# Gate projections as narrow fp32 strips, and the context stream moved behind the latent stream in the opening of a hybrid layer

## The chip, the cores and the metric

The kernel runs on one core of one Trainium2 chip. The metric is the device time of one execution, in microseconds. Three runs of the kernel before took 936.86, 937.15 and 937.77 us, so the median is 937.15 us.

## The reference, cut to what matters

One layer of a diffusion backbone works on 512 latent tokens (`x`, 512 by 1024) and 256 context tokens (`ctx`, 256 by 1024). Everything is float32. What the change touches is the opening of the layer:

```python
mod   = silu(c)     @ w_ada + b_ada            # shift, scale, gate vectors of the latents
mod_c = silu(c_ctx) @ w_ada + b_ada            # the same for the context
h  = rms_norm(x,   g_norm1) * (1 + sc1)  + sh1
hc = rms_norm(ctx, g_norm1) * (1 + csc1) + csh1
aq, ak, av, dq, dk, dv, dz, da, db, ga, gd = split_cols(h @ w_in)      # and the same of hc
beta = sigmoid(db)                             # 16 columns: 2 directions x 8 heads
g    = -exp(a_log) * softplus(da + dt_bias)    # 16 columns
q, k, v = silu(conv3(dq, dk, dv)); k = l2_normalize(k) ...
# gated delta rule in chunks of 64 tokens, forward and backward, the context's final state into the latents;
# windowed attention beside it; both gated, projected, then an MLP of width 4096
```

`da` and `db` are the gate projections: 16 columns each of a combined projection of 4896 columns. `dk` has 512 columns, four tiles of 128, and its latents and context tokens both go through a short convolution, a SiLU and a normalization before the triangular matrices of the delta rule can be built.

## The kernel before, in words

Activations lie transposed: 128 channels on the partitions, tokens along the free axis, eight channel groups (`KT = 8`). A projection to 128 output columns is a tile. Each weight tile (512 KB) is loaded raw, then split into a rounded part (`hi`, line 240, ScalarE) and the rest (`lo`, line 241, VectorE); activations are split the same way (lines 295 and 296). `mm3` (lines 289 to 291) adds three fp32r products per channel group: hi by hi, hi by lo, lo by hi. So a tile of the latents is 24 products of 512 columns, and its context part 24 products of 256 columns. They accumulate in PSUM, which has eight banks of 512 columns, handed out in a ring; `bank(2)` takes two neighbours.

The opening. `NONES` products of a matrix of ones (line 188) come first. The latents (`xT`, four loads of 512 KB) and context (`ctxT`, two) are squared (line 265, ScalarE), added up on VectorE (lines 269 and 273) and summed over the partitions by a product with ones (line 276); a Ln and an Exp give the reciprocal root. `ada(kt)` computes shift and scale of channel group `kt` as a row: two loads of 512 KB of `w_ada`, and for each four products of 32 output rows by 256 columns (line 207) that lie side by side in the array's four column groups; in plain fp32 each product shows as two records. `columns(kt)` copies the row out (line 221), turns it into columns with two small products (line 226) and forms `modA` and `modS` (lines 229 and 230). `modulate` then does, for latents and for context, a product with the reciprocal root and the scale on VectorE (line 294), the rounded part with the shift added on ScalarE (line 295) and the rest on VectorE (line 296).

Three tiles are early: the gate tile (`T_AB`, where 32 of 128 columns are in use) and the first two tiles of `dk`. Their products run inside the loop over channel groups, for latents and context, as each group is modulated:

```python
early, EARLY = [], {T_AB: 0, T_DK: 0, T_DK + 1: 0}
        if kt + AHEAD < KT:
            columns(kt + AHEAD, ada(kt + AHEAD))
        for (w, acc), k0 in zip(early, EARLY.values()):
            for k in range(kt + 1) if kt == k0 else (kt,):
                mm3(acc[:, :512], w, [hx[k]], ...)
                mm3(acc[:, 512:768], w, [hc[k]], ...)
```

After the loop come constants, then the gates (lines 601 to 624: a chain of small operations on ScalarE and VectorE over 768 tokens on 16 partitions that ends in `gb` at line 622), the other two tiles of `dk`, the convolutions (lines 573 to 575), the SiLU of all four, and the products that bring `gb` into token order (line 649). From there `mats` (normalization, line 591, then the chunk matrices, lines 699 to 731) runs woven with the projections for attention, and the triangular matrices are inverted row by row on VectorE.

The order of each engine's instructions is fixed when the kernel is built: the framework's planner takes, for every engine, the ready instruction that stands earliest in the program, by its own estimate of durations, and puts in the waits. A NoSync dependency (`tc.add_manual_dep`) adds an order without a semaphore. `act` keeps activations that share a function table together: a group with another table starts after all of the group before. All loads are issued by SyncE in one queue. SBUF outside the pools is a ring of 167 units of 256 columns (`alloc`); a reused unit makes the next writer wait for its last reader. Raw weight tiles have four buffers, split ones two.

## Time and profile before

| | |
|---|---|
| median of three runs | 937.15 us (936.86 to 937.77) |
| the profiled execution's own time | 938.35 us |
| its span, first to last instruction | 936.5 us |
| TensorE (PE) busy | 901.0 us, 96% |
| VectorE (DVE) busy | 596.2 us, 64% |
| ScalarE (ACT) busy | 443.0 us, 47% |
| mean granted clock of TensorE | 0.991 |

Busy time of PE is not PE at its peak, since products overlap and their ends are modelled: how long a product costs is read from the distance between the starts of neighbours. PEld are the weight loads that run beside. DMA share 1.0 means that all 16 DMA engines had work all the time. PEclk is the granted clock: 1.00 is 2.4 GHz and 0.50 is 1.2 GHz.

### The profile page before, as it was taken

What the parts mean: (1) busy time and instruction counts of PE and PEld (TensorE: products, weight loads), DVE (VectorE), ACT (ScalarE), POOL (GpSimd) and SP (SyncE); (2) the same over time, 40 slices, a digit from 0 to 9 for tenths busy, and PEclk for the clock granted to TensorE, in tenths of its full rate; (3) what the DMA queues carried; (4) which work ended last, traced back from release to release, by engine and by line L of the source; (5) the groups of instructions that cost most, each with busy time, mean ns of one, the idle gap of its engine ahead of it and who ended that gap; (6) DMA issues with size and microseconds to landing.
All of it is one profiled execution on the core that took longest, in us unless ns stands there. A gap on an engine that the chain in (4) does not pass through costs nothing.

```text
span 936.5 us, 18158 instructions
## 1 busy us (share of the span) xinstructions
PE 901.0 (96%) x7736; PEld 730.0 (78%) x7736; DVE 596.2 (64%) x1013; ACT 443.0 (47%) x815; POOL 12.1 (1%) x26
## 2 busy tenths in 40 slices
PE   7999889999999999989999998999999999999998
PEld 5688667877777677778888888988888888888886
DVE  4666779997877998358875977982454235434411
ACT  5467635338567887475555434660243125213400
POOL 0000000000000001000000000000000000000000
PEclk8999989999999999999999999999999999999999
DMA  9921111210000132225424474481344124222111
GB/s 350 347 69 46 47 47 46 68 46 24 23 11 24 34 114 92 93 92 162 157 86 136 157 273 137 143 291 39 115 152 138 45 68 156 92 67 91 45 43 47
DMA packets 29600, 98.72 MB, mean 105 GB/s; under 512 B 3664, under 2 KB 4176, under 8 KB 29520
## 3 DMA queue, kind: packets, MB, share of 16 engines
q1 hardware_dynamic: 29520, 97.57, 31.5%
q8 instruction: 60, 0.98, 0.4%
q14 instruction: 20, 0.16, 0.1%
HBM read 95.46 MB, written 2.10 MB: 104 GB/s over the span
## 4 chain that ended last, share of the span: by engine, by line
PE 72%; DVE 12%; ACT 8%; DMA 4%; issue 3%; SPq 0%; DVEq 0%; ACTq 0%
PE banks L289 16%; PE banks L290 15%; PE banks L291 15%; PE banks L943 9%; PE banks L988 2%; DMA wr<-in_wm 2%; PE banks L1055 2%; DMA wa<-in_wada 2%; DVE wl L241 1%; ACT m L146 1%; PE banks L1086 1%; PE banks L1067 1%; PE banks L526 1%; DVE m L183 1%; PE banks L207 1%
## 5 line engine op out<-in xcount | busy, mean ns | idle before, releaser
L289 PE MATMUL banks<-m,m 128*128 128x512 f32 (+1 forms) x584 | 219.4, 379 | 3.4 <-ACT m L240 3.0
L290 PE MATMUL banks<-m,m 128*128 128x512 f32 (+1 forms) x584 | 219.0, 377 | 0.1
L291 PE MATMUL banks<-m,m 128*128 128x512 f32 (+1 forms) x584 | 218.9, 377 | 0.0
L240 ACT ACTIVATE m<-wr 128x1024 fp32r<-128x1024 f32 x67 | 70.8, 1058 | 157.9 <-PE banks L290 78.9
L289 PEld LDWEIGHTS banks<-m,m 128*128 128x128 f32 x584 | 109.2, 188 | 26.4 <-ACT m L240 3.1
L241 DVE TENSOR_TENSOR m<-wr,m 128x1024 fp32r<-128x1024 f32 x67 | 81.9, 1224 | 70.3 <-PE banks L290 34.2
L290 PEld LDWEIGHTS banks<-m,m 128*128 128x128 f32 x584 | 109.5, 188 | 21.7 <-DVE m L241 0.8
L291 PEld LDWEIGHTS banks<-m,m 128*128 128x128 f32 x584 | 109.3, 188 | 21.2 <-issue 0.8
L289 PE MATMUL banks<-m,wh 128*128 128x512 f32 (+1 forms) x312 | 114.1, 366 | 0.9 <-DVE m L1270 0.6
L291 PE MATMUL banks<-m,wl 128*128 128x512 f32 (+1 forms) x312 | 111.5, 360 | 2.3 <-DVE wl L241 2.3
L290 PE MATMUL banks<-m,wh 128*128 128x512 f32 (+1 forms) x312 | 111.0, 356 | 0.0
L943 PE MATMUL banks<-m,wh 128*128 128x512 f32 x320 | 103.9, 399 | 0.0
L1371 DVE SCALAR_TENSOR_TENSOR m<-banks,modT,m 128x512 f32<-128x512 f32 x32 | 24.0, 750 | 101.0 <-PE banks L291 101.0
L241 DVE TENSOR_TENSOR wl<-wr,wh 128x1024 fp32r<-128x1024 f32 (+1 forms) x60 | 64.7, 1079 | 28.4 <-ACT wh L240 28.2
L240 ACT ACTIVATE wh<-wr 128x1024 fp32r<-128x1024 f32 (+1 forms) x60 | 56.6, 944 | 31.5 <-PE banks L290 15.0
L943 PEld LDWEIGHTS banks<-m,wh 128*128 128x128 f32 x320 | 59.1, 188 | 12.1
L291 PEld LDWEIGHTS banks<-m,wl 128*128 128x128 f32 x312 | 58.8, 189 | 11.3 <-DVE wl L241 3.0
L289 PEld LDWEIGHTS banks<-m,wh 128*128 128x128 f32 x312 | 59.3, 190 | 10.4 <-DVE m L1270 0.8
L290 PEld LDWEIGHTS banks<-m,wh 128*128 128x128 f32 x312 | 59.3, 190 | 7.5 <-issue 0.2
L943 PE MATMUL banks<-m,wl 128*128 128x512 f32 x160 | 65.0, 406 | 0.0
L182 ACT ACTIVATE m<-m 128x512 fp32r<-128x512 f32 (+1 forms) x56 | 35.2, 631 | 48.9 <-DVE m L1354 21.1
L183 DVE TENSOR_TENSOR m<-m,m 128x512 fp32r<-128x512 f32 (+1 forms) x56 | 38.3, 689 | 18.8 <-ACT m L182 18.3
(231 smaller groups left out, 1274.7 us busy)
## 6 DMA issues: line engine op xcount, KB each, us to landing
wr<-in_wm SPq DMA_DIRECT2D x64, 512.0 KB, 3.5
wr<-in_win SPq DMA_DIRECT2D x39, 512.0 KB, 3.5
wa<-in_wada SPq DMA_DIRECT2D x32, 512.0 KB, 4.0
m<-in_wada SPq DMA_DIRECT2D x16, 512.0 KB, 10.2
m<-in_xT SPq DMA_DIRECT2D x8, 512.0 KB, 6.1
wr<-in_wbr SPq DMA_DIRECT2D x16, 256.0 KB, 2.7
wr<-in_wout SPq DMA_DIRECT2D x8, 512.0 KB, 4.7
out<-m SPq DMA_DIRECT2D x8, 256.0 KB, 2.0
```

The lines of the kernel that those rows point to most:

```text
L146: r = A.activation(out_, in_, func, **kw)
L182: A.activation(r32(hi), src, AF.Copy)
L183: (eng or V).tensor_tensor(r32(lo), src, hi, op=ALU.subtract)
L240: A.activation(r32(hi), raw, AF.Copy)
L241: V.tensor_tensor(r32(lo), raw, hi, op=ALU.subtract)
L289: PE.matmul(acc, w[0][:, k, :], xhi, start=(start and i == 0), stop=False)
L290: PE.matmul(acc, w[0][:, k, :], xlo, start=False, stop=False)
L291: PE.matmul(acc, w[1][:, k, :], xhi, start=False, stop=(stop and i == n - 1))
L943: PE.matmul(acc.ap, w[x][:, k, :], hx[k][y], start=(k == p == 0), stop=(k == KT - 1 and p == 2))
L988: PE.matmul(pa.ap, w[x][:, j, :], r32(Q[y][:, :, j, :]), start=(j == p == 0), stop=(j == 3 and p == 2))
L1055: PE.matmul(z[r, x * 256 + q * HD:x * 256 + (q + 1) * HD], src[q][r, col(c):col(c) + CH], S[r, q * HD:(q + 1) * HD], start=True, stop=True)
L1371: V.scalar_tensor_tensor(xn_[ct], acc.ap, modT[:, 3, ct:ct + 1], xn_[ct], op0=ALU.mult, op1=ALU.add)
```

## The change

- The gate tile is gone from the list of tiles. Its 32 used columns become a weight `wab` of 128 KB. For each channel group one plain fp32 product of 32 output rows is formed; four groups lie side by side in the four column groups of the array and give four partial sums in one bank, which ScalarE and VectorE add up later, with `da` and `db` on 32 neighbouring partitions. ScalarE writes an fp32 copy of each modulated group for it.
- All four tiles of `dk` are early, one bank each, and only their latents are multiplied beside the modulation. The context's loads, sum of squares, modulation and products come behind it.
- `w_ada` comes in loads of 1 MB; the sums of squares are added up by TensorE from four parts; `NONES` falls from 36 to 16, and three and six products of ones stand around the first row and its columns (`WARM`).
- The gates' chain is moved behind the convolutions of `dk`, and the queue of weight tiles starts ahead of the constants.

```diff
-NONES = 36
+CTXAT = 7
+WARM = 3, 6
+NONES = 16
 AHEAD = 2
...
+        wb = alloc(2048)
+        nc.sync.dma_start(out=wb.ap, in_=I["wada1"][kt])
         for half in range(2):
-            wb = alloc(1024)
-            nc.sync.dma_start(out=wb.ap, in_=I["wada1"][kt, half])
             for g in range(4):
...
+    def warm(bank_, n):
+        for _ in range(n):
+            PE.matmul(bank_[:, 384:512], ones, ones, start=True, stop=True)
...
+    ebufs = [alloc(1024) for _ in range(8)]
...
     def columns(kt, rp_):
+        if kt == 0:
+            warm(rp_, WARM[0])
         rb_ = alloc(256)
-        A.activation(rb_.ap, rp_[:, :256], AF.Copy)
+        row_[kt] = A.activation(rb_.ap, rp_[:, :256], AF.Copy)
...
+        if kt == 0:
+            warm(mp_, WARM[1])
         mp_.free()
...
-        A.activation(r32(hi), raw, AF.Copy)
+        h = A.activation(r32(hi), raw, AF.Copy)
+        if not early:
+            tc.add_manual_dep(h.ins, row_[0].ins.name, nosync, reason="behind the first row")
...
-    early, EARLY = [], {T_AB: 0, T_DK: 0, T_DK + 1: 0}
+    early, EARLY = [], {T_DK: 0, T_DK + 1: 0, T_DK + 2: 0, T_DK + 3: 1}
...
-    columns(0, ada(0))
-    for k4 in range(KT // 4):
-        nc.sync.dma_start(out=cs_[:, k4 * 1024:(k4 + 1) * 1024], in_=I["ctxT"][k4])
-    load_early()
...
+    def rms(src, nt, n, r):
+        ss = bank()
         for i in range(nt):
             b = alloc(1024)
             A.activation(b.ap, src[:, i * 1024:(i + 1) * 1024], AF.Square)
+            w = 512
+            while w >= n:
+                V.tensor_tensor(b[:, :w], b[:, :w], b[:, w:2 * w], op=ALU.add)
+                w //= 2
+            PE.matmul(ss[:, :n], ones, b[:, :n], start=(i == 0), stop=(i == nt - 1))
+            b.free()
...
+    rms(xs_, 4, SEQ, rx)
+    columns(0, ada(0))
+    wab_ = alloc(256)
+    wab = wab_.ap.rearrange("p (k c) -> p k c", k=KT)
+    raw0 = wfetch(I["win"][T_DK])
+    tx, tc_ = [], []
+    def ab_strips(ab, hs, s):
+        for g in range(4):
+            m = PE.matmul(ab[32 * g:32 * g + 32], wab[:, 4 * s + g], hs[g][0].ap, start=(s == 0), stop=(s == 1))
+            tc.add_manual_dep(m.ins, hs[3][1].ins.name, nosync, reason="strips together")
+        for _ in range(4):
+            hs.pop(0)[0].free()
...
     for kt in range(KT):
...
+        h = alloc(512)
+        tx.append((h, A.activation(h.ap, t.ap, AF.Identity, bias=modS[:, kt, 0:1])))
         t.free()
+        if kt == 0:
+            load_early(raw0)
+            load_early(raw1)
         if kt + AHEAD < KT:
             columns(kt + AHEAD, ada(kt + AHEAD))
+        if kt + AHEAD == CTXAT:
+            nc.sync.dma_start(out=wab_.ap, in_=I["wab"])
+            for k4 in range(KT // 4):
+                nc.sync.dma_start(out=cs_[:, k4 * 1024:(k4 + 1) * 1024], in_=I["ctxT"][k4])
         if len(early) < len(EARLY):
             load_early()
         for (w, acc), k0 in zip(early, EARLY.values()):
             for k in range(kt + 1) if kt == k0 else (kt,):
-                mm3(acc[:, :512], w, [hx[k]], start=(k == 0), stop=(k == KT - 1), ks=[k])
-                mm3(acc[:, 512:768], w, [hc[k]], start=(k == 0), stop=(k == KT - 1), ks=[k])
+                mm3(acc.ap, w, [hx[k]], start=(k == 0), stop=(k == KT - 1), ks=[k])
+    abx = bank()
+    for s in range(2):
+        ab_strips(abx.ap, tx, s)
+    rms(cs_, 2, CTX, rc)
+    for kt in range(KT):
+        t = alloc(256)
+        o = kt * 512
+        hc.append(modulate(t.ap, ct_[kt], rc, modA[:, kt, 1:2], modS[:, kt, 1:2],
+                           HCb[:, o:o + 256], HCb[:, o + 256:o + 512]))
+        tc_.append((t, A.activation(t.ap, t.ap, AF.Identity, bias=modS[:, kt, 1:2])))
+    abc = bank()
+    for s in range(2):
+        ab_strips(abc[:, :CTX], tc_, s)
...
-    for q in range(4):
-        kv_tile(T_DK + q, 4 + q, kT[q])
+    for q, (w, acc) in enumerate(early):
+        conv(kT[q][:, :SEQ], acc.ap, 4 + q)
+        acc.free()
+        acc = bank()
+        mm3(acc[:, :CTX], w, hc)
+        conv(kT[q][:, SEQ:TOK], acc[:, :CTX], 4 + q)
+        acc.free()
...
+    for src, cols in ((abx, slice(0, SEQ)), (abc, slice(SEQ, TOK))):
+        n = cols.stop - cols.start
+        A.activation(ad[:, cols], src[0:32, :n], AF.Identity, bias=dtb[0:32])
+        for g in range(1, 4):
+            V.tensor_tensor(ad[:, cols], ad[:, cols], src[32 * g:32 * g + 32, :n], op=ALU.add)
+        src.free()
```

The rest of the gates' chain stays as it was, on 32 partitions for `da` and `db` together.

## Rows read from the trace of the kernel before

**Rows 1.** The page: busy time, share of the span and instructions by engine.

```profile
PE 901.0 (96%) x7736; PEld 730.0 (78%) x7736; DVE 596.2 (64%) x1013; ACT 443.0 (47%) x815; POOL 12.1 (1%) x26
```

**Rows 2.** Windows: busy us by engine (instructions), granted clock, DMA share, GB/s.

```profile
0.00:20.00 20.00, 13.80 (x94) 11.37 (x94) 7.45 (x18) 11.72 (x15) 0.21 (x4) 0.87 0.89 340
20.00:40.00 20.00, 18.60 (x121) 10.17 (x121) 13.32 (x27) 8.26 (x15) 0.00 (x0) 0.87 0.93 363
40.00:60.00 20.00, 20.00 (x152) 16.02 (x149) 12.08 (x30) 8.13 (x16) 0.00 (x0) 1.00 0.40 141
60.00:80.00 20.00, 20.00 (x115) 17.26 (x114) 12.91 (x19) 15.74 (x21) 1.47 (x2) 1.00 0.25 80
80.00:100.00 20.00, 20.00 (x262) 15.63 (x260) 11.98 (x24) 13.91 (x24) 0.00 (x0) 1.00 0.09 28
100.00:120.00 20.00, 15.26 (x427) 11.74 (x426) 18.29 (x31) 12.50 (x23) 0.00 (x0) 0.93 0.18 54
...
140.00:160.00 20.00, 18.96 (x91) 14.82 (x90) 19.88 (x34) 10.55 (x17) 0.00 (x0) 1.00 0.08 27
```

**Rows 3.** One window of 1 us in the opening, same columns.

```profile
25.00:26.00 1.00, 1.00 (x8) 0.34 (x7) 0.00 (x0) 0.63 (x2) 0.00 (x0) 0.99 1.05 418
```

**Rows 4.** Timeline, 1 to 42 us: start, duration, engine, line, operation, idle before.

```profile
1.06 9.95 PE L188 MATMUL banks<-ones 128*128 128x128 f32 x72 [1.06 <-DVE ones L156]
...
12.00 0.64 PE L207 MATMUL banks<-m,m 128*32 128x256 f32 x8 [1.00 <-DMA m<-in_wada]
...
18.11 0.75 DVE L294 SCALAR_TENSOR_TENSOR m<-m,modA,m 128x512 f32<-128x512 f32 x1
...
18.90 0.72 ACT L295 ACTIVATE m<-m,modS 128x512 fp32r<-128x512 f32 x1
...
20.62 0.79 PE L289 MATMUL banks<-m,m 128*128 128x512 f32 x1 [2.99 <-ACT m L240]
...
31.52 0.39 PE L289 MATMUL banks<-m,m 128*128 128x512 f32 x1
...
31.75 0.39 PE L290 MATMUL banks<-m,m 128*128 128x512 f32 x1
...
40.09 0.38 ACT L221 ACTIVATE m<-banks 128x256 f32<-128x256 f32 x1 [0.44 <-PE banks L207]
...
41.36 0.28 DVE L229 TENSOR_SCALAR modA<-banks,bada,c_prm 128x2 f32<-128x2 f32 x1 [0.93 <-PE banks L226]
```

**Rows 5.** Timeline at 47 us: narrow products, a group of strips, what follows.

```profile
47.03 0.28 PE L289 MATMUL banks<-m,m 128*128 128x256 f32 x1
...
47.15 0.28 PE L290 MATMUL banks<-m,m 128*128 128x256 f32 x1
...
47.47 1.07 PE L207 MATMUL banks<-m,m 128*32 128x256 f32 x16
...
48.47 0.19 PEld L289 LDWEIGHTS banks<-m,m 128*128 128x128 f32 x1 [0.41 <-issue]
```

**Rows 6.** Timeline, 61 to 87 us: gates' chain, and what comes behind.

```profile
61.36 1.00 DVE L612 TENSOR_SCALAR m<-banks,c_prm 16x768 f32<-16x768 f32 x1 [0.53 <-PE banks L291]
...
70.96 0.60 DVE L622 TENSOR_SCALAR m<-m,nega 16x768 f32<-16x768 f32 x1
...
80.39 1.57 PE L649 MATMUL banks<-c_prm,m 64*64 64x16 f32 x48
...
83.15 0.85 ACT L146 ACTIVATE m<-m 128x768 f32<-128x768 f32 x1 [1.01 <-DVE m L575]
...
84.19 1.28 ACT L142 ACT_TABLE_LOAD   x1
...
86.72 1.06 ACT L146 ACTIVATE m<-banks,epsc 128x512 f32<-128x512 f32 x2
```

**Rows 7.** Groups by line and shape to 105 us: one context modulation step on ACT, DVE.

```profile
L295 ACT ACTIVATE m<-m,modS 128x256 fp32r<-128x256 f32 x8 | 4.0, 497 | 0.4 <-DVE m L294 0.4
...
L294 DVE SCALAR_TENSOR_TENSOR m<-m,modA,m 128x256 f32<-128x256 f32 x8 | 3.8, 477 | 0.0
```

More of the change, by code (lines that the diff above doesn't have):

```diff
@@ L265, in tile_layer @@
             A.activation(b.ap, src[:, i * 1024:(i + 1) * 1024], AF.Square)
-            if tot is None:
-                tot = b
-            else:
-                V.tensor_tensor(tot.ap, tot.ap, b.ap, op=ALU.add)
-                b.free()
-        w = 512
-        while w >= n:
-            V.tensor_tensor(tot[:, :w], tot[:, :w], tot[:, w:2 * w], op=ALU.add)
-            w //= 2
-        ss = bank()
-        PE.matmul(ss[:, :n], ones, tot[:, :n], start=True, stop=True)
-        tot.free()
+            w = 512
[4 more added lines that the diff above has]
+            b.free()
         act(r, ss[:, :n], AF.Ln, bias=epsc, scale=1.0 / D)
         ss.free()
-    for r in (rx, rc):
         act(r, r, AF.Exp, scale=-0.5)
+    rms(xs_, 4, SEQ, rx)
[10 more added lines that the diff above has]
+            hs.pop(0)[0].free()
     def mm3(acc, w, xs, start=True, stop=True, ks=None):
@@ L363, in in_tile_steps @@
     def in_tile_steps(ti, with_ctx):
-        for (_, e), t in zip(early, EARLY):
-            if t == ti:
-                return e
         w = wnext()
@@ L599, in l2n @@
         t.free()
-    nega = const.tile([16, 1], F32, name="nega")
-    act(nega, alog[0:16], AF.Exp)
-    V.tensor_scalar(nega, nega, -1.0, None, op0=ALU.mult)
-    gb = alloc(TOK)
-    acc = in_tile(T_AB, True)
-    V.memset(gb[0:64], 0.0)
-    t, t2 = alloc(TOK), alloc(TOK)
-    ad, mx, be = t[0:16], t2[0:16], gb[32:48]
-    V.tensor_scalar(ad, acc[0:16, :TOK], dtb[0:16], None, op0=ALU.add)
-    V.tensor_scalar(mx, ad, 0.0, None, op0=ALU.max)
-    act(be, acc[32:48, :TOK], AF.Exp, scale=-1.0)
-    acc.free()
-    act(be, be, AF.Ln, bias=onec[32:48])
-    act(be, be, AF.Exp, scale=-1.0)
-    A.activation(ad, ad, AF.Abs)
-    act(ad, ad, AF.Exp, scale=-1.0)
-    act(ad, ad, AF.Ln, bias=onec[0:16])
-    V.tensor_tensor(mx, mx, ad, op=ALU.add)
-    V.tensor_scalar(gb[0:16], mx, nega, None, op0=ALU.mult)
-    t.free()
-    t2.free()
     def kv_tile(ti, ci, dst):
@@ L632, in tile_layer @@
     kT = [alloc(TOK, True) for _ in range(4)]
-    for q in range(4):
-        kv_tile(T_DK + q, 4 + q, kT[q])
+    for q, (w, acc) in enumerate(early):
[5 more added lines that the diff above has]
+        acc.free()
+    for b in ebufs:
+        b.free()
+    nega = const.tile([32, 1], F32, name="nega")
+    act(nega, alog[0:32], AF.Exp)
+    V.tensor_scalar(nega, nega, -1.0, None, op0=ALU.mult)
+    gb = alloc(TOK)
+    t, t2 = alloc(TOK), alloc(TOK)
+    ad, mx, be = t[0:32], t2[0:32], gb[32:64]
+    for src, cols in ((abx, slice(0, SEQ)), (abc, slice(SEQ, TOK))):
[4 more added lines that the diff above has]
+        src.free()
+    V.tensor_scalar(mx, ad, 0.0, None, op0=ALU.max)
+    act(be, ad, AF.Exp, scale=-1.0)
+    act(be, be, AF.Ln, bias=onec[32:64])
+    act(be, be, AF.Exp, scale=-1.0)
+    A.activation(ad, ad, AF.Abs)
+    act(ad, ad, AF.Exp, scale=-1.0)
+    act(ad, ad, AF.Ln, bias=onec[0:32])
+    V.tensor_tensor(mx, mx, ad, op=ALU.add)
+    V.tensor_scalar(gb[0:32], mx, nega, None, op0=ALU.mult)
+    t.free()
+    t2.free()
     for q in range(4):
```

69 lines of the change are left out of this document (33 added, 36 removed).

## The prediction, on record before the changed kernel ran

> **What bounds the kernel now.** I read the page first: PE is busy for 901.0 of 936.5 us [rows 1]. Time can come from two places only: products that go away, or stretches in which PE waits or runs slowly. The windows show where these lie, and the timeline of the opening why.
>
> In the first 20 us PE is busy for 13.8 us, in the next 20 for 18.6, and then solidly until 100 us [rows 2]. The mean granted clock is 0.87 in both of the first windows; with two levels, 1.0 and 0.5, that is 0.13 x 20 x 2 = 5.2 us at 1.2 GHz in each, some 10 us in all, and rows 3 show full speed again from 25 us. The loads run without a break there: at 25 us the DMA share is full at 418 GB/s [rows 3]. The first tile product starts at 20.62 us, having waited 2.99 us for a weight split on ACT [rows 4]. What ACT and DVE did instead was the sum of squares of the context, whose loads stand ahead of the second channel group. From about 31 us neighbours start 0.23 us apart (512 columns) [rows 4] and 0.12 us apart (256 columns) [rows 5]: that is PE at its peak. So up to 31 us the opening is bound by the chain load, row, columns, modulation; from there to 100 us by PE; and from 100 to 160 us PE falls to 15.26 and 18.96 of 20 us while DVE stands at 18.29 and 19.88 [rows 2]. That stretch is bound by DVE and begins with the normalization of `kT`, whose first Ln is at 86.72 us [rows 6].
>
> **The change, part by part.** All against the profiled execution, 938.35 us (span 936.5); the median of the runs is 1.2 us lower, so I subtract the same gain from 937.15.
>
> *The gate tile.* It leaves 24 products of 0.23 and 24 of 0.12 us: 8.4 us on PE. It comes back as 8 fp32 products of 512 and 8 of 256 columns. Rows 5 show a group of exactly this kind: 16 records (two rounds of four strips, 256 columns) in 1.07 us, then 0.41 us before the next weight load. So context strips cost 1.07 + 0.41, latent strips twice the columns, 2.1 + 0.41: 4.0 us. If wide strips do not overlap at all, eight products of 512 columns at four passes (four times 0.23) are 7.4, the whole is about 11 us and the loss 2.9 (a round of rows 5, 0.53, is as long as four products of 0.12, hence four passes); the least is 3.2 without the pauses. I take **-4.4**, as rows 5 are the same form with half the columns.
>
> *The opening.* The loads ahead of the modulation are in order: latents 2.1 MB, then `w_ada` 1.05 MB per group, a weight tile of 0.52 behind each of the first four. At 412 GB/s or so (1.27 us per 0.52 MB) and with the first half load of `w_ada` in at 12.0 us [rows 4], groups 0 to 7 land at 13.3, 17.1, 20.9, 24.7, 28.5, 31, 33.6 and 36 us, the context at 38 to 39. From landing to the first tile product stand the strips (1.07), row copy and columns (1.27, from the copy's start to the first DVE step), two small DVE steps (0.28 each), 0.75 on DVE and 0.72 on ACT [rows 4, 5], about 4.4 us; for group 0 the three products of ones ahead of the row copy add 0.8 (36 take 9.95 us, 0.28 each [rows 4]). So products of group 0 start at 18.5 us, or at about 20 if the clock is still at half there, against 20.62; but then groups follow at 21.5, 25, 29 us, because ACT and DVE no longer work on the context. By 28.5 us the first three tiles have had three groups: 27 products, 6.3 us, and four groups of strips are done. Before, by 30.8 us, I count 7 wide and 4 narrow tile products, 2.1 us, and three groups of strips. From either point PE has more than it can do: four tiles ask 2.8 us per group and strips and columns 2, against 2.5 us of loading. So the gain is 2.3 us of time, 4.2 of products and 1.6 of strips: **-8**. Bounds: -2 (only the 2.99 us wait goes, with extra copies on ACT in its place) and -9. The 20 products of ones that go were over at 11 us, ahead of the first `w_ada` load [rows 4]: nothing. The fp32 copies, eight of 0.72 us on ACT, lie beside PE's backlog, where ACT has 8 of 20 us in use [rows 2]; without that cover they would cost up to 5.8.
>
> *Loads of 1 MB.* They cost the early half of the first one, 1.3 us, already counted. SyncE's queue now holds a load of twice the size, and more of the ring is held (weights, copies): the load of group 7 needs units that group 3's modulation has just read. That is at about 30 us, when its turn comes, so I cost it at nothing; if it came late, context and constants behind it in the queue would be late by as much.
>
> *The context behind.* PE takes ready instructions in program order, so the context's sum of squares is taken when the latents are through. From 28.5 us that is 2.1 (fourth tile, groups 0 to 2) + 14 (groups 3 to 7) + 7.2 (strips and columns) + 2.5 (latent gate strips): about 54 us. Then two products with ones (0.9), Ln, Exp and one modulation: PE waits some **+2.5 to 3**. Then channel groups come at the pace of ACT, two steps of 0.5 us each (DVE: two of 0.48) [rows 7]: eight take 8 us, to 65 us. In that time PE has the context of the first `dk` tiles, 0.35 us per tile and group; three tiles fill it. Their banks are freed by the convolutions, which ACT and DVE do while PE sums squares. All four tiles are through at about 70 us, against 80.39 [rows 6]: PE is **10.4 us ahead** (4.4 + 8 less 2 to 3, rounding aside).
>
> *The gates' chain.* It needs the last context group, so it starts at 66 us. Before, it took from 61.36 to 71.56 us, 10.2 us [rows 6]; six additions and one more ACT step replace one addition, of which about 0.9 us stands behind the last strip: `gb` at 77. The SiLU of `kT` is in the next table group: from the last Ln at about 75.4 one table load of 1.28, four SiLU of 0.85, another table load [rows 6]: the first Ln of the normalization at 81.4 us, against 86.72. So the stretch bound by DVE begins only **5.3 us** earlier.
>
> Between 5.3 and 10.4: PE can use its lead on attention tiles until weights (two split buffers) and banks run out, about one tile; some of it is then lost in the DVE-bound stretch. I take 7.
>
> **A rule to weigh.** The Trainium skill (TensorEngine Tiling, Performance Considerations, PSUM Bottleneck) says that packing speeds up TensorE but not the emptying of PSUM, which can then become the limit. No row of before shows strips emptied by additions; its consequence here would be a gates' chain that ends last, and the price of that is worked out below from rows.
>
> **The rivals.**
>
> *Likeliest (0.50):* as summed, gain 7, 930.2 us; alone it spans 927 to 933.
>
> *All of PE's lead comes through (0.27):* gain 10.4 to 13, if the context's sum is taken in a hole of PE ahead of 54 us, so that hardly any wait is left: about 925.5. For it: PE dense from 40 to 100 us [rows 2], so the lead counts fully there. Against it: DVE at 19.88 of 20 us later [rows 2].
>
> *The gates' chain ends last (0.13), slower:* in the program it stands behind the convolutions. If the fixed order keeps it there, it starts when the last `dk` tile's context is through and convolved (1.4 us: three steps of about 0.48 by the nearest row of rows 7): at 71.5 us if PE is through at 70, at 76.4 if the convolutions free banks late, so that only the first tile fills PE up to 65 us and 1.5 + 8.4 us follow. From its start 11.1 us lead to `gb` and 4.4 more to the first Ln: 87 to 92 us against 86.72. The DVE-bound stretch then begins 0.3 to 5 us later than before and swallows all that PE gained; I take 2.4, 939.5 us. It decides when the chain starts after 71.2 us. For it: ACT is in use for 15.74 of 20 us from 60 to 80 us already [rows 2]. Against it: the strips are ready at 66 us, while the later convolutions still wait for PE, and DVE has 7 us free there [rows 2].
>
> *The opening does not start earlier (0.10):* the clock stays at half to 25 us, tiles begin as late as before, and what is left is 4.4 less the 3 us junction and 1 us of chain: 936.8.
>
> **How the numbers follow.** 930.2 is the likeliest case. About 0.2%, 1.9 us, is what these runs can tell from no change. Faster: 0.50 + 0.27 + a part of the last rival, 0.82; the same: 0.08; slower: most of the gates' chain, 0.10. A range of 922.5 to 936.5 leaves out the gates' chain, half of the last rival and the far end of the second.
>
> **What would show it.** Right: first tile product of `dk` at 18 to 20 us; starts 0.23 us apart from 29 us; latent strips 2.1 us; a PE wait on ACT of 2 to 3 us between 52 and 58 us; the products that bring `gb` into token order at 76 to 78 us, the first Ln at 81 us; from 100 to 160 us more PE idle than the 5.8 us of the two windows of rows 2. Wrong: a `w_ada` load that waits for a buffer; several waits of PE on ACT between 55 and 70 us; strips one after the other; a first Ln behind 86.7 us.

## The result, and the profile after

The changed kernel takes 941.75 us (median of 20 runs, 939.22 to 943.89); the kernel before, on the same chips, 937.87 us (20 runs). The ratio is 1.0037, 95% interval 1.0026 to 1.0049: slower by 3.5 us, where 7 us less were forecast. The profiled execution of the changed kernel took 939.99 us, with a span of 937.9 us.

The page of the changed kernel, busy time by engine, against [rows 1]:

```profile
PE 900.3 (96%) x7706; PEld 724.5 (77%) x7706; DVE 595.2 (63%) x1017; ACT 451.6 (48%) x832; POOL 12.1 (1%) x26
```

PE is busy for 0.7 us less only. Where it is idle has moved, as the windows of the changed kernel show (columns as in [rows 2]):

```profile
0.00:20.00 20.00, 15.85 (x100) 10.45 (x100) 6.59 (x19) 11.89 (x16) 0.21 (x4) 1.00 0.90 351
20.00:40.00 20.00, 17.23 (x121) 10.47 (x121) 10.05 (x19) 8.83 (x14) 0.00 (x0) 1.00 0.64 246
40.00:60.00 20.00, 17.92 (x114) 12.22 (x114) 11.93 (x24) 11.04 (x18) 0.73 (x1) 1.00 0.75 272
60.00:80.00 20.00, 16.99 (x119) 14.92 (x120) 16.64 (x35) 12.66 (x28) 0.73 (x1) 0.83 0.17 60
80.00:100.00 20.00, 17.37 (x147) 13.83 (x145) 7.92 (x17) 18.11 (x28) 0.00 (x0) 0.90 0.00 1
...
140.00:160.00 20.00, 19.65 (x91) 15.31 (x90) 19.91 (x33) 9.97 (x16) 0.00 (x0) 0.99 0.09 27
```

Against [rows 2], the first 40 us run at full clock (1.00 against 0.87), as hoped. But between 40 and 100 us, where PE was solid before, it is now idle for 7.7 us (2.08, 3.01 and 2.63), and from 60 to 100 us the granted clock is 0.83 and 0.90: 3.4 and 2.0 us lost at half clock.

As the mark for the stretch bound by DVE I take the transpose right ahead of the row-by-row inversion (the prediction let that stretch begin earlier, with the normalization). Another transpose stands 5 us ahead of it. Here is the mark in the timeline of the kernel before, then of the changed one:

```profile
145.55 2.22 DVE L752 STREAM_TRANSPOSE m<-m 128x1024 f32<-128x1024 f32 x1
```

```profile
146.73 2.21 DVE L798 STREAM_TRANSPOSE m<-m 128x1024 f32<-128x1024 f32 x1
```

From there to the end of the execution the time hardly differs: 938.35 - 145.5 = 792.9 us before, 939.99 - 146.7 = 793.3 after. I call this moment S; in these two executions the difference lies ahead of it. One window from 0 to S (before, then after) says what fills that time:

```profile
0.00:145.50 145.50, 130.65 (x1489) 99.50 (x1490) 96.51 (x175) 82.55 (x131) 1.68 (x6) 0.94 0.40 146
```

```profile
0.00:146.70 146.70, 127.92 (x1456) 92.73 (x1457) 95.50 (x179) 90.47 (x147) 1.68 (x6) 0.94 0.39 142
```

S can be split into PE's idle time, what half clock costs (estimated as (1 - clock) times the window), and what is left, PE's work at full speed. Before: 14.8 + 8.7 + 122 us. After: 18.8 + 8.8 + 119. The idle time is read from the trace: the change added 4 us of waiting. The half clock that it saved in the opening came back later. The last term is rough. In the kernel half_loads (below) nearly the same number of PE's instructions stands ahead of S, and yet it comes out as 141.6 - 15.9 - 1.4 = 124 us:

```profile
0.00:141.60 141.60, 125.73 (x1459) 88.88 (x1460) 95.89 (x179) 90.89 (x148) 1.68 (x6) 0.99 0.41 147
```

So 3 us less of work are less than what this split can tell.

**Where PE waits now.** First the loads. SyncE's waits in the changed kernel from 10 to 42 us (waiting line, releaser, us in total, times, longest):

```profile
SPq L206 <- DVE m L320: 8.4, 2, 4.5
SPq L206 <- PE banks L210: 7.7, 2, 6.2
SPq L206 <- DMA m<-in_wada: 4.8, 2, 3.6
SPq L206 <- PE banks L239: 4.5, 2, 2.9
```

L206 issues the 1 MB loads of `w_ada`. The last four of the eight, from 13.87 us on, wait for units of the ring, held above all until the modulation (L320) and the strips (L210) of earlier groups have read them. Two rows of SyncE's timeline show what that does to the context, and three windows the DMA engines meanwhile:

```profile
13.87 24.18 SPq L206 DMA_DIRECT2D m<-in_wada  x4
...
38.56 1.28 SPq L343 DMA_DIRECT2D m<-in_ctxT  x2
```

```profile
25.00:30.00 5.00, 3.75 (x26) 2.42 (x29) 2.86 (x5) 2.61 (x4) 0.00 (x0) 1.00 0.72 300
30.00:35.00 5.00, 4.74 (x31) 3.34 (x24) 2.86 (x5) 2.67 (x4) 0.00 (x0) 1.00 0.59 210
35.00:40.00 5.00, 5.00 (x47) 2.88 (x46) 1.46 (x4) 1.53 (x3) 0.00 (x0) 1.00 0.22 57
```

The context's loads were forecast to have landed by 38 to 39 us; they are issued at 38.56, while the DMA engines stand at 0.22 to 0.72 (1.05 before at 25 us, [rows 3]).

From the second on, the channel groups do not wait for these loads. The eight loads land at 12.3, 16.1, 19.9, 24.3, 27.9, 30.4, 35.4 and 42.6 us (issue plus time to landing), and the strips of the eight groups start at 12.73, 18.16, 23.81, 29.46, 35.34, 38.83, 42.56 and 46.52 us. What sets their distance of 5.4 to 5.9 us up to 35 us is PE's order: the strips of a group stand behind the products of the group before. PE of the changed kernel:

```profile
23.81 1.07 PE L210 MATMUL banks<-m,m 128*32 128x256 f32 x16
...
28.09 0.74 PE L313 MATMUL banks<-m,m 128*128 128x512 f32 x2 [1.03 <-ACT m L319]
...
29.46 1.07 PE L210 MATMUL banks<-m,m 128*32 128x256 f32 x16
```

From the strips at 23.81 us the chain leads over the row copy (24.95), the columns (25.61) and the modulation (27.32) to the group's first product at 28.09, for which PE waits; only then come the next strips, whose load had landed 5 us before. Another order was not tried.

Then the context itself. Timeline of the changed kernel, 54 to 65 us, PE, ACT and DVE:

```profile
54.74 1.99 ACT L611 ACTIVATE m<-banks,c_prm 128x512 f32<-128x512 f32 x3 [2.41 <-PE banks L315]
...
55.93 1.92 PE L302 MATMUL banks<-m,m 128*32 128x512 f32 x16
...
57.01 2.00 ACT L281 ACTIVATE m<-m 128x1024 f32<-128x1024 f32 x2 [0.29 <-PE banks L302]
...
59.93 0.67 PE L286 MATMUL banks<-m,ones 128*128 128x256 f32 x2 [2.08 <-DVE m L284]
...
61.53 0.79 PE L286 MATMUL banks<-m,ones 128*128 128x256 f32 x2 [0.93 <-DVE m L284]
62.35 0.47 ACT L148 ACTIVATE m<-banks,epsc 128x256 f32<-128x256 f32 x1 [1.25 <-PE banks L286]
...
63.84 1.31 ACT L319 ACTIVATE m<-m,modS 128x256 fp32r<-128x256 f32 x3 [0.56 <-DVE m L318]
64.40 1.01 PE L313 MATMUL banks<-m,m 128*128 128x256 f32 x3 [2.08 <-ACT m L319]
```

When the latent strips are through at 57.85 us, the context's squares (L281) are only under way, though their loads landed at 45.4 and 46.7. On ACT and DVE they stand among convolutions (L611 and its fellows), and the last thing they waited for were units that the strips read (L302, 0.29 us). PE waits three times, 2.08 + 0.93 + 2.08 us, and runs at half clock from 62 us on: narrow products start 0.21 us apart (67.77, 67.98 us), where [rows 5] have 0.12.

Last the gates' chain, of ACT and DVE, 73 to 95 us:

```profile
73.40 0.46 ACT L665 ACTIVATE m<-banks,c_prm 32x256 f32<-32x256 f32 x1 [2.39 <-PE banks L302]
...
76.15 0.86 DVE L667 TENSOR_TENSOR m<-m,banks 32x256 f32<-32x256 f32 x2
...
77.89 0.42 DVE L667 TENSOR_TENSOR m<-m,banks 32x256 f32<-32x256 f32 x1
78.41 0.85 ACT L148 ACTIVATE m<-m 32x768 f32<-32x768 f32 x1 [0.18 <-DVE m L667]
...
84.33 1.28 ACT L144 ACT_TABLE_LOAD   x1
85.33 0.61 DVE L677 TENSOR_SCALAR m<-m,nega 32x768 f32<-32x768 f32 x1
85.63 3.04 ACT L148 ACTIVATE m<-m 128x768 f32<-128x768 f32 x4
...
88.86 1.28 ACT L144 ACT_TABLE_LOAD   x1
...
94.32 1.05 ACT L148 ACTIVATE m<-banks,epsc 128x512 f32<-128x512 f32 x2 [1.13 <-PE banks L629]
```

The first Ln of the normalization starts at 94.32 us, against 86.72 in [rows 6]; `gb` is ready at 85.94 instead of 71.56.

### The profile page after: what moved, and what is told of

It reads as the page before. It is cut to its first block, busy times and chain, and to the rows that moved or that the text cites. A ratio compares the mean times of both kernels' runs of the same rounds, so it can differ in the third digit from the quotient of the medians.

```text
span 937.9 us, 18101 instructions
## 1 busy us (share of the span) xinstructions
PE 900.3 (96%) x7706; PEld 724.5 (77%) x7706; DVE 595.2 (63%) x1017; ACT 451.6 (48%) x832; POOL 12.1 (1%) x26
## 4 chain that ended last, share of the span: by engine, by line
PE 76%; DVE 12%; ACT 7%; DMA 3%; issue 2%; SPq 0%; DVEq 0%; ACTq 0%
PE banks L313 16%; PE banks L314 16%; PE banks L315 16%; PE banks L989 10%; PE banks L1034 2%; PE banks L1101 2%; DMA wa<-in_wada 2%; PE banks L564 1%; PE banks L1132 1%; PE banks L1113 1%; DVE wl L262 1%; ACT m L148 1%; PE banks L570 1%; DVE m L819 1%; DVE m L818 1%
## 5 line engine op out<-in xcount | busy, mean ns | idle before, releaser
L313 PE MATMUL banks<-m,m 128*128 128x512 f32 (+1 forms) x600 | 224.2, 379 | 5.1 <-ACT m L319 4.6
L314 PE MATMUL banks<-m,m 128*128 128x512 f32 (+1 forms) x600 | 225.2, 378 | 0.0
L315 PE MATMUL banks<-m,m 128*128 128x512 f32 (+1 forms) x600 | 225.2, 378 | 0.0
L313 PEld LDWEIGHTS banks<-m,m 128*128 128x128 f32 x600 | 112.8, 190 | 27.6 <-ACT m L319 6.6
L314 PEld LDWEIGHTS banks<-m,m 128*128 128x128 f32 x600 | 113.2, 190 | 22.4 <-issue 1.2
L315 PEld LDWEIGHTS banks<-m,m 128*128 128x128 f32 x600 | 113.1, 189 | 21.8 <-issue 1.6
L313 PE MATMUL banks<-m,wh 128*128 128x512 f32 (+1 forms) x280 | 102.8, 368 | 0.3 <-ACT wh L259 0.2
L315 PE MATMUL banks<-m,wl 128*128 128x512 f32 (+1 forms) x280 | 100.4, 361 | 1.5 <-DVE wl L262 1.4
L314 PE MATMUL banks<-m,wh 128*128 128x512 f32 (+1 forms) x280 | 101.6, 363 | 0.0
L262 DVE TENSOR_TENSOR wl<-wr,wh 128x1024 fp32r<-128x1024 f32 (+1 forms) x58 | 62.3, 1073 | 25.8 <-ACT wh L259 25.6
L259 ACT ACTIVATE wh<-wr 128x1024 fp32r<-128x1024 f32 (+1 forms) x58 | 54.5, 940 | 30.0 <-PE banks L314 16.2
L989 PEld LDWEIGHTS banks<-m,wh 128*128 128x128 f32 x320 | 59.1, 188 | 12.2
L315 PEld LDWEIGHTS banks<-m,wl 128*128 128x128 f32 x280 | 53.3, 191 | 9.7 <-DVE wl L262 2.3
L313 PEld LDWEIGHTS banks<-m,wh 128*128 128x128 f32 x280 | 53.4, 191 | 8.8 <-ACT wh L259 0.7
L314 PEld LDWEIGHTS banks<-m,wh 128*128 128x128 f32 x280 | 53.5, 191 | 7.0 <-issue 0.4
L185 DVE TENSOR_TENSOR m<-m,m 128x512 fp32r<-128x512 f32 (+1 forms) x56 | 38.3, 689 | 18.8 <-ACT m L184 18.3
```

Of the source, the lines that this page charges most:

```text
L185: (eng or V).tensor_tensor(r32(lo), src, hi, op=ALU.subtract)
L259: h = A.activation(r32(hi), raw, AF.Copy)
L262: V.tensor_tensor(r32(lo), raw, hi, op=ALU.subtract)
L313: PE.matmul(acc, w[0][:, k, :], xhi, start=(start and i == 0), stop=False)
L314: PE.matmul(acc, w[0][:, k, :], xlo, start=False, stop=False)
L315: PE.matmul(acc, w[1][:, k, :], xhi, start=False, stop=(stop and i == n - 1))
```

## The experiments

Eleven kernels, each compared with runs of the kernel before on the same chip. "N" is the first product of the normalization (line 591 of before), S the start of the DVE-bound stretch, both from the profiled execution; "rest" is that execution's time less S; the clock is the median over the runs.

| kernel | median us | ratio to before (95%) | clock | N | S | rest |
|---|---|---|---|---|---|---|
| before | 937.87 | 1 | 0.992 to 0.994 | 81.9 | 145.5 | 792.9 |
| changed | 941.75 | 1.0037 (1.0026 to 1.0049) | 0.987 | 93.3 | 146.7 | 793.3 |
| ctx_two_groups_earlier | 944.17 | 1.0087 (1.0066 to 1.0108) | 0.989 | 95.8 | 150.3 | 794.0 |
| gates_ahead_of_convolutions | 937.39 | 1.0006 (0.9994 to 1.0017) | 0.992 | 91.6 | 144.3 | 792.8 |
| half_loads | 936.99 | 0.9995 (0.9979 to 1.0011) | 0.993 | 90.2 | 141.6 | 791.4 |
| strips_alone | 938.27 | 1.0020 (1.0007 to 1.0034) | 0.988 | 83.0 | 141.0 | 795.8 |
| ctx_earlier_own_squares | 942.46 | 1.0039 (1.0023 to 1.0056) | 0.990 | 93.4 | 147.4 | 793.0 |
| half_loads_gates_first | 935.58 | 0.9975 (0.9961 to 0.9989) | 0.996 | 89.6 | 142.0 | 793.2 |
| ctx_earlier_half_loads_gates_first | 937.06 | 0.9985 (0.9970 to 0.9999) | 0.994 | 80.4 | 147.3 | 792.7 |
| no_context_sum | 938.73 | 1.0002 (0.9985 to 1.0019) | 0.991 | 89.8 | 143.7 | 793.2 |
| no_gates_chain | 936.57 | 0.9987 (0.9969 to 1.0004) | 0.990 | 82.4 | 142.5 | 792.2 |
| half_loads_gates_first_no_sum | 926.74 | 0.9890 (0.9860 to 0.9921) | 0.996 | 76.4 | 133.0 | 792.1 |
| ctx_one_earlier_half_loads_gates_first | 932.91 | 0.9949 (0.9933 to 0.9965) | 0.996 | 81.0 | 139.8 | 793.6 |

What one edit is worth is the difference of two ratios times 938 us. By the intervals such a difference is good to about 2 us, to 3 with half_loads_gates_first_no_sum. N and S belong to one execution: that of half_loads (932.99 us) is 4.0 us below its median, that of ctx_earlier_half_loads_gates_first (939.96) 2.9 above, the others lie within 2.1. In eleven of the twelve executions other than before's, the rest lies between 791.4 and 794.0 us, so an execution's time goes with its S.

**Context two groups earlier.**

```diff
-CTXAT = 7
+CTXAT = 5
```

> The changed kernel with one number changed: the context's loads stand behind the sixth... that is, CTXAT is 5 instead of 7, so they are issued after w_ada of group 5 and not after group 7. Theory A (the context comes too late: its sum of squares, its modulation and with them the gates' chain start only when the latents are through): the sum is done some 15 us earlier, PE has no long wait between 57 and 65 us, gb ends at 72 to 77 instead of 85.9 us, the first Ln of the normalization at 78 to 83 instead of 94.3 us, and the time falls to 928 to 934 us, 0.4 to 1% under the kernel before. Rival B (the opening is held back by the ring of buffers, loads waiting): nothing of this helps, the loads of groups 6 and 7 come 2.5 us later and the time is that of the changed kernel, 940 to 944. Rival C (the gates' chain is late because it stands behind the convolutions): gb ends only 2 to 4 us earlier, 938 to 941.

Slower by 4.7 us than the changed kernel, nearest to the second expectation. The context's loads came earlier and the first square by 7 us, but the second only by 0.9 us, and the sum's Ln by 0.5 (61.85 against 62.35). Timeline of this kernel, ACT:

```profile
50.01 1.06 ACT L281 ACTIVATE m<-m 128x1024 f32<-128x1024 f32 x1 [1.79 <-PE banks L302]
...
57.10 1.06 ACT L281 ACTIVATE m<-m 128x1024 f32<-128x1024 f32 x1 [1.75 <-PE banks L302]
```

Each square waits for a unit that a group of strips (L302) has just read: the fp32 copies hold the ring. An earlier load alone buys nothing. What it costs is not the loads of `w_ada` (the last is issued at 37.90 us, 37.7 in the changed kernel) but the order: the strips of the seventh group stand at 46.63 instead of 42.56 us, a square ahead of its modulation, and the latents are through at 60.10 instead of 57.85.

**Gates' chain ahead of the convolutions** (only the order in the program).

```diff
-    kT = [alloc(TOK, True) for _ in range(4)]
-    for q, (w, acc) in enumerate(early):
...
     V.tensor_scalar(gb[0:32], mx, nega, None, op0=ALU.mult)
...
+    kT = [alloc(TOK, True) for _ in range(4)]
+    for q, (w, acc) in enumerate(early):
...
```

> The changed kernel with the gates' chain put ahead of the convolutions of the dk tiles in the program, as before the change; nothing else. Rival C (order of the chain): gb ends 5 to 8 us earlier than in the changed kernel (at 78 to 81 us), the first Ln at 87 to 90 us, time 935 to 938. Theory A (the context is late whatever stands behind it): the chain can't start before the last context strips at 73 us, gb ends at 83 to 85, the convolutions come later by what the chain takes on ACT, and the time stays within 2 us of the changed kernel, 940 to 943.

Worth 2.9 us: the time is that of the first expectation, the chain that of the second. Its start doesn't move (its ScalarE step after the last context strips is at 73.49 us, 73.40 in the changed kernel) and `gb` hardly does (85.06); the first Ln is 1.65 us earlier (92.67). The convolutions were in its way, but what makes it late is the context.

**Loads of 512 KB.**

```diff
-        wb = alloc(2048)
-        nc.sync.dma_start(out=wb.ap, in_=I["wada1"][kt])
         for half in range(2):
+            wb = alloc(1024)
+            nc.sync.dma_start(out=wb.ap, in_=I["wada1"][kt][:, half * 1024:(half + 1) * 1024])
             for g in range(4):
...
-        wb.free()
+            wb.free()
```

> The changed kernel with w_ada in loads of 512 KB into buffers of 4 units, as before the change; nothing else. Rival B (1 MB loads wait for room in the ring): the loads are issued earlier, the DMA share between 25 and 40 us goes up from 0.2 to 0.7 to 0.9, the groups follow at less than 5.7 us, and the time falls by 2 to 4 us to 937 to 939. Theory A: the groups come a little earlier, but PE had enough to do with the latents from 30 us on, and the context is behind them in any case: within 1 us of the changed kernel, 940 to 943.

Worth 3.9 us by the ratios, as the first expectation had it. Windows of this kernel:

```profile
25.00:30.00 5.00, 4.33 (x29) 2.29 (x29) 2.87 (x5) 2.66 (x4) 0.00 (x0) 1.00 1.03 409
30.00:35.00 5.00, 5.00 (x35) 3.28 (x27) 2.86 (x5) 2.67 (x4) 0.00 (x0) 1.00 0.73 281
```

The DMA share is 1.03 and 0.73 where the changed kernel had 0.72 and 0.59; the context's loads are issued at 34.93 instead of 38.56 us. The Trainium skill (DMA: Bandwidth & Descriptors, Bandwidth) says to batch transfers to 1 MiB or more. Here the smaller loads move more (409 against 300 GB/s from 25 to 30 us). The 1 MB loads are not slow in flight (423 and 418 GB/s from 15 to 25 us in the changed kernel); they start late, and SyncE's waits from 10 to 42 us fall from 27.3 to 20.9 us in all. The measurement decides.

The gain is not made by the latents. The second halves of the strips still come 5.2 to 5.5 us apart (19.12, 24.57, 29.82 and 35.28 us), and the latents are through at 58.61 us, 0.8 later than in the changed kernel. What comes earlier is the context: its loads land at 40.5 and 41.8 us, and its squares run ahead of the strips instead of behind units that the strips hold. ACT of this kernel:

```profile
48.92 1.05 ACT L280 ACTIVATE m<-m 128x1024 f32<-128x1024 f32 x1
...
52.27 1.04 ACT L280 ACTIVATE m<-m 128x1024 f32<-128x1024 f32 x1
```

Behind the latents PE then waits once, 2.82 us up to 62.49, instead of three times. Which of the two did it, the earlier landing or other units of the ring, was not separated.

**Strips alone**: the kernel before with the gate tile as strips and the third `dk` tile early in its place, context and loads as before.

```diff
-    early, EARLY = [], {T_AB: 0, T_DK: 0, T_DK + 1: 0}
+    early, EARLY = [], {T_DK: 0, T_DK + 1: 0, T_DK + 2: 0}
...
+        h, g = alloc(512), alloc(256)
+        tx.append((h, A.activation(h.ap, t[:, :512], AF.Identity, bias=modS[:, kt, 0:1])))
+        tc_.append((g, A.activation(g.ap, t[:, 512:768], AF.Identity, bias=modS[:, kt, 1:2])))
```

> The kernel before with one part of the change: the gate tile becomes fp32 strips (latents and context, behind the loop over the groups), the third dk tile takes its place among the early tiles with its context, the gates' chain stands where it did. The order of loads, sums and context is that of before. The strips save 4.4 us on PE by the sum of the prediction. Theory A (the loss is in the context's place, the strips are good): 932 to 936 us, 0.2 to 0.6% under before. Rival D (the strips lose: partial sums, copies on ACT, the chain behind them): 938 to 942 us; then latent strips take more than 2.1 us or gb ends later than 71.6 us.

S is 4.5 us earlier than before; by the rough split above that is 3.4 us less work (118.5) and less half clock. Yet over all runs this kernel is slower than before by 1.9 us, in the range of the second expectation. That one's sign came true too: `gb` ends at 75.41 us, later than 71.56. But the first Ln (86.93, before 86.72) and S do not follow it, so the late `gb` is not what costs. It is the one execution whose rest is longer, by 2.9 us, and one window of it (first) against the same of before shows where:

```profile
200.00:220.00 20.00, 17.90 (x325) 13.51 (x325) 15.18 (x24) 15.83 (x32) 2.07 (x4) 0.83 0.10 33
```

```profile
200.00:220.00 20.00, 18.43 (x336) 14.05 (x337) 18.60 (x35) 14.81 (x31) 2.07 (x4) 1.00 0.17 54
```

A clock of 0.83 over 20 us is 3.4 us lost. Over all runs its clock is 0.988 against 0.994 of before. Why this kernel falls to half clock there was not tried, so that the strips alone make the kernel faster is not shown.

**Context two groups earlier, with two buffers of its own for its squares** (CTXAT 5 as above, and):

```diff
+    csq = [alloc(1024) for _ in range(2)]
...
-            b = alloc(1024)
+            b = own[i] if own else alloc(1024)
...
-    rms(cs_, 2, CTX, rc)
+    rms(cs_, 2, CTX, rc, csq)
```

> The changed kernel with the context's loads two groups earlier (CTXAT 5) and the context's squares in two buffers of their own instead of units of the ring. With the earlier loads alone the squares waited for the latent strips (50.0 and 57.1 us), because their units in the ring still held the fp32 copies that the strips read. Theory A2 (the late context is made by that wait): squares at 33 to 36 us, the sum's products among the latents' at 45 to 52 us, no wait of PE above 2 us between 57 and 66 us, gb ends at 72 to 78 us, the first Ln at 82 to 87 us, time 930 to 936 us. Rival E (the context's modulation and its products, not the sum, set the pace: eight steps of ACT and DVE each 0.9 us and four narrow tiles): the hole goes, but gb ends at 80 or later and the time stays at 938 to 942. Rival B (ring too tight, 34 units instead of 42): loads of w_ada come later than in the changed kernel and the latents end behind 58 us; 941 to 945.

No gain (+0.2 us). The squares now run at 40.05 and 43.53 us and wait for no unit, but the second product with ones still comes at 59.46 and the Ln at 60.24: the wait for units was not the only one. That product's additions end at 45.76 us; on PE it stands behind the last latent strips (58.47), which are themselves 1.7 us later than in the changed kernel.

**Loads of 512 KB and gates first, together.**

> The changed kernel with w_ada in 512 KB loads and the gates' chain ahead of the convolutions, both as before the change. Alone they took 4.8 and 4.4 us off the changed kernel's 941.75. If they are two separate costs (ring in the opening, order of the chain), the sum is 932 to 934 us. If both only move the same late chain (gb, then the first Ln), the second adds little: 936 to 938.

5.8 us less than the changed kernel, within the intervals the two gains added (6.8), between its two expectations, and faster than both kernels. PE's wait behind the latents is the same as with the smaller loads alone:

```profile
62.91 0.80 PE L312 MATMUL banks<-m,m 128*128 128x256 f32 x3 [2.82 <-ACT m L318]
```

**The same with the context two groups earlier and its own square buffers.**

> All three together: context loads two groups earlier with squares of their own, 512 KB loads, gates ahead of the convolutions. Theory A2: the context's sum is done before the latents end, gb ends at 70 to 75 us, the stretch bound by DVE begins 5 to 9 us earlier than before the change (its first transpose at 137 to 141 us against 145.5), and the time is 928 to 933 us, under both kernels. Rival F (PE and DVE are both near their limit from 120 us on, so an earlier chain is given back): 934 to 938 us.

The normalization's first product is 9.2 us earlier (80.4), yet the kernel is not faster, as the second expectation had it, and in the profiled execution (its slowest) S is 5.3 us later. From 80 us to S that execution loses 6.7 us at half clock and 6.7 to idle PE, against 1.9 and 6.0 without the earlier context. So an early normalization alone doesn't set S; PE's waits and clock up to S count too.

**The context's sum left out.** Its reciprocal root is set to 1; the loads stay.

```diff
+    V.memset(rc, 1.0)
...
-    rms(cs_, 2, CTX, rc)
```

> The changed kernel without the context's sum of squares: its reciprocal root is set to 1, so squares, additions, two products with ones, a Ln and an Exp are left out, and the context's modulation waits only for its loads and its columns. It shows what the late sum costs. Theory A2: the modulation of the context is done among the latents (44 to 56 us), PE has no wait above 2 us behind the latent strips, gb ends at 72 to 78 us; time 931 to 936. Rival C (the order behind it costs more than the sum): gb ends at 79 to 83 us, 937 to 940.

3.3 us less than the changed kernel, with `gb` at 83.71 us: about what the second expectation said. Windows of this kernel:

```profile
60.00:80.00 20.00, 19.98 (x145) 17.27 (x144) 15.13 (x28) 10.87 (x21) 0.73 (x1) 1.00 0.30 109
80.00:100.00 20.00, 14.69 (x125) 10.08 (x123) 8.53 (x17) 17.54 (x27) 0.00 (x0) 0.83 0.00 1
```

PE's hole behind the latents is gone (19.98, at full clock, against 16.99 at 0.83), and a new one stands 20 us later (14.69 against 17.37), again followed by half clock. ACT is at 17.54 there: PE now waits for the gates' chain and normalization. A lead of PE alone is given back.

**The gates' chain left out**: `gb` gets constants, the strips are formed but not read.

```diff
-    for src, cols in ((abx, slice(0, SEQ)), (abc, slice(SEQ, TOK))):
...
-    V.tensor_scalar(gb[0:32], mx, nega, None, op0=ALU.mult)
+    V.memset(gb[0:32], -0.1)
+    V.memset(gb[32:64], 0.5)
```

> From the changed kernel. The gates' chain is left out: gb gets two constants, the strips are still formed but nothing reads them. So the additions, the steps with Exp and Ln and one table load fall away (73.4 to 85.3 us in the changed kernel), and the SiLU of kT can follow the last convolution at once. Theory (the chain is what delays the normalization, and with it the stretch bound by DVE): first Ln of the normalization at 83 us or earlier instead of 94.3, stretch bound by DVE starts at 138 to 142 us instead of 146.7, median 932 to 936 us. Rival (the context's late arrival holds kT itself: the last dk tile is through at 79.4 us, convolution and SiLU follow, and the chain fits beside them): first Ln at 88 us or later, stretch starts at 145 us or later, 939.5 us or more. In either case the time should be the start of that stretch plus 793 us.

Worth 4.7 us; S is 4.2 us earlier, the first Ln at 85.73. That lies between the two expectations: the chain does hold the stretch, but with it gone `kT`'s own convolutions, which wait for the context, let the first Ln come only 1 us ahead of [rows 6].

**Loads of 512 KB, gates first, and the context's sum left out.**

> The changed kernel with both undone parts (loads of 512 KB, gates' chain ahead of the convolutions), and the context's reciprocal root set to 1, its sum of squares left out. Theory (each of the three costs time of its own in the opening, and the two undone parts only move the bound to the context's sum): 2 to 4 us below the kernel with both undone, about 932 us, stretch bound by DVE at 139 to 140 us. Rival (the sum lies off the path once the loads are early; PE's hole is given back in front of the DVE-bound stretch): within 1 us of the kernel with both undone, 935 to 936.5 us, stretch at 141.5 to 142.5 us.

8.0 us less than with the sum, twice the upper end of what was expected. Timeline of this kernel, ACT and DVE:

```profile
52.93 1.70 ACT L319 ACTIVATE m<-m,modS 128x256 fp32r<-128x256 f32 x4
...
61.66 3.13 DVE L656 TENSOR_TENSOR m<-m,banks 32x512 f32<-32x512 f32 x6
...
72.56 0.60 DVE L666 TENSOR_SCALAR m<-m,nega 32x768 f32<-32x768 f32 x1
...
79.69 1.06 ACT L148 ACTIVATE m<-banks,epsc 128x512 f32<-128x512 f32 x2
```

Here the context is modulated right behind the latents, at 52.93 us. The strips are added up from 61.66 us, `gb` is ready at 73.16 and the first Ln starts at 79.69, 7 us ahead of [rows 6]. Its window up to S shows PE's idle time at 10.3 us and no half clock:

```profile
0.00:133.00 133.00, 122.68 (x1452) 87.80 (x1453) 92.86 (x177) 86.88 (x143) 1.69 (x6) 1.00 0.44 157
```

That is the course that the prediction had drawn, with the gain that its second case named (926.74 us against 925.5), though without the work of the sum. What separates the changed kernel from it are three things: the sum, the loads, the chain's place. Their single gains (3.3 + 3.9 + 2.9 us) make 10.1, together they make 13.8; that difference is within what the intervals leave. Clear of them is the sum: 3.3 us alone, 8.0 with the other two undone. As long as something else is late, it hides part of what the sum costs. And that cost is not PE's wait, which was 2.82 us: without the sum the chain's ScalarE step after the last context strips is at 60.84 instead of 71.62 us.

**Loads of 512 KB, gates first, the context one group earlier (CTXAT 6) with its own square buffers.** Nothing is left out here.

> The changed kernel with loads of 512 KB, the gates' chain ahead of the convolutions, the context's loads one channel group earlier (CTXAT 6) and two buffers of their own for its squares. Theory (the context's late arrival still costs 1 to 3 us once the two parts are undone): 933 to 935 us, stretch bound by DVE at 140 to 141 us. Rival (as with two groups earlier: squares on ACT and loads of the context take the place of a modulation step, and nothing is won): 935.5 to 937.5 us, stretch at 142 us or later.

The best complete version: 932.91 us, 0.5% below the kernel before. The squares of the context now lie beside the latents' products (the second at 48.52 us) and the sum's Ln follows at 56.68 us:

```profile
48.52 1.04 ACT L282 ACTIVATE m<-m 128x1024 f32<-128x1024 f32 x1
...
56.68 0.48 ACT L148 ACTIVATE m<-banks,epsc 128x256 f32<-128x256 f32 x1
```

In half_loads_gates_first the second square is at 52.69 and that Ln at 60.90. One group earlier earns 2.4 us by the ratios, just clear of the intervals; two groups earlier cost 0.9, within them. So the moment of the context's loads seems to count.

## Why the prediction was wrong, point by point

*The opening* is the first step that failed. It held for the first group (first tile product of `dk` at 17.73 us, 18 to 20 forecast), for the clock (no half clock up to 60 us) and for the landing of the first six loads. What failed is "but then groups follow at 21.5, 25, 29 us, because ACT and DVE no longer work on the context": the chain of a group was to start when its load lands, but in PE's order its strips stand behind the products of the group before. The groups' first products came at 22.33, 28.09 and 33.75 us, PE was idle for 2.8 us from 20 to 40 us, and the latents were through at 57.85 instead of 54 us. The smaller loads leave this as it is (22.86, 28.30, 33.94), so it is not the loads; that another order would mend it is argued, not tried.

*The gate tile* held nearly: latent strips 1.92 us (2.1 forecast), context strips 0.64 us for a round (0.53). Of the 4.4 us the kernel with the strips alone shows 3.4 in the rough split up to S, and nothing in its time.

*Loads of 1 MB* is the second: "when its turn comes, so I cost it at nothing". The last four loads waited for ring units, whose readers were late with the groups, and the context's loads were issued when they should have landed. The prediction had named that condition itself ("context and constants behind it in the queue would be late by as much"). Undone, this is 3.9 us, and the runs show by what path: not by earlier groups, but by squares of the context that no longer stand behind the strips.

*The context behind* failed most. Its sum was costed at a PE wait of 2.5 to 3 us; measured are 2.08 + 0.93 + 2.08. What was counted is the chain product, Ln, Exp, modulation; what was not is that the squares and their additions must be done by then, and that they share ring units with the fp32 copies and ACT and DVE with the convolutions. With the squares out of the way (half_loads) the wait is 2.82 us, as forecast. In the changed kernel the context's first modulation step started at 63.84, 6 us behind the latents, not 3, and a stretch of half clock went with it. PE's first attention product came at 79.43 against 80.39 before, a lead of 1 us instead of 10.4.

*The gates' chain* began at 73.40 instead of 66 us, 3.8 of it from the latents' end, 3 from the sum. Then it took 12.5 us to `gb` (11.1 forecast) and 8.4 us more to the first Ln (4.4). The two table loads and four SiLU steps were in the forecast and took what it said; at nothing stood what comes behind the second table load, which ends at 90.14 us: two Exp of the gates, three squares of `kT` (2.31 us) and a product, 4.2 us in all. 7.4 + 1.4 + 4.0 make the 12.9 us between 81.4 and 94.32, but for rounding. The third case had named this end: a chain that starts after 71.2 us turns the change slower, 939.5 us; it came at 73.40, and 941.75 us. Only its reason was half right: order behind the convolutions is worth 2.9 us, but it was the late context that moved the start. The rule that was weighed there (the Trainium skill, TensorEngine Tiling, PSUM Bottleneck: packing does not speed up emptying PSUM) is not what made the chain end last: the six additions take 3.13 us where they stand in one piece, and only two rows of them, 0.86 and 0.42 us, stood behind the last strips.

*What is left with the loads and the chain undone* can be read in half_loads_gates_first (935.58 us, 930.2 forecast). The latents are through at 59.03 us, 5 later than forecast; the chain starts at 71.62, 5.6 later; `gb` follows after 10.7 us (11.1 forecast) and the first Ln after 8.3 more (4.4). So the late latents and the steps ahead of that Ln remain.

*Between 5.3 and 10.4 I take 7* rests on a lead of PE that counts by itself. (The 10.4 takes the sum's wait at 2 us; at its own 2.5 to 3 it would be 9.4 to 9.9.) No_context_sum shows that it doesn't: PE's hole was closed and opened again ahead of the normalization.

Of its signs of being wrong three came: a `w_ada` load that waits for a buffer, several waits of PE between 55 and 70 us, a first Ln behind 86.7 us.

What stays open: S is not tied to the first normalization product alone, and which of the products woven in between 80 us and S wait for what was not taken apart; nor whether the half clock there follows from the shape of the work or varies from run to run. The smaller parts of the change (fewer products of ones, those around the first row, sums of squares from four parts, the queue of weight tiles ahead of the constants) were not undone one by one.

## What to carry to other kernels

When work is moved behind a stream, list all that must have been done before it can start (loads, buffers, squares, partial sums), and ask of each whether it truly lies beside the stream; the moved part begins when the last of them ends. A load of twice the size in a shared ring waits until twice the space is free, so a queue that was never idle can begin to wait; then ask who waits for it, since it need not be the reader of the load itself but what stands behind it in the queue. Whether a chain starts when its data land must be read from the order of its engine. And a lead of one engine is worth only what the next engine's chain lets through: sum idle time, slow clock and work up to the start of the next bound stretch, and compare that start between kernels before the end.

## What the runs showed of the hardware that I had not expected

A hole of PE can cost twice. In the changed kernel, which waits three times between 57.85 and 64.40 us, narrow products ran at 0.21 instead of 0.12 us until about 68.6 us, a mean clock of 0.83 from 60 to 80 us: up to 3.4 us beside the hole itself. Not every hole did so: in ctx_one_earlier_half_loads_gates_first PE waits once, 2.35 us up to 69.05, and the clock from 60 to 80 us is 1.00. Over the runs of the complete kernels the medians go roughly with the clock: 0.987 in the changed kernel, 0.992 to 0.994 before, 0.996 in the two that beat it most clearly; a step of 0.001 over 935 us is about 0.9 us, so by this estimate the clock alone could make some 5 us between the changed kernel and before, if none of it fell into waits. Whether it is a cause or goes with the waits is not shown. Runs of one kernel spread likewise: half_loads from 932.89 us at 0.998 to 939.96 at 0.991.
